# Cross attention's value projection in one sweep of 512 moving columns, and three side loads of the feed-forward stage queued behind weight loads

## The chip, the cores and the metric

The kernel runs on one core of a Trainium2 chip. The metric is the device time of one execution in microseconds (us); less is better. Every number of the trace comes from one profiled execution.

## What is computed

One inference step of a decoder trunk of one layer, for a prompt of 256 tokens and a batch of 8 single-token samples that share the parameters (264 token columns in all, D_MODEL 2048). Three sub-layers follow one another: attention beside a state-space scan, cross attention into 256 memory tokens, and a feed-forward block with a short convolution. The change lies in the second, with a small part in the third. The prompt's side of the second, cut to what matters (`rms_norm` scales a row by the inverse root of its mean square):

```
q = rms_norm(rms_norm(x, g) @ w_cq)      # 4 heads of 128
k = rms_norm(rms_norm(mem, g_mem) @ w_ck)
v = rms_norm(mem, g_mem) @ w_cv          # 256 memory tokens, 2048 -> 512
p = softmax(q @ k.T * scale)             # per head, 256 x 256
x = x + (p @ v) @ w_co                   # 512 -> 2048
```

The samples do the same with cached keys and values of their own.

## The kernel before, in words

TensorE works on float32 data as float32r. To keep the precision, every operand of a projection is split in two: `hi`, the value rounded to float32r, and `lo`, the rest. One logical product is then three matmul passes, hi by hi, hi by lo and lo by hi (`mm3`, L97 to L100). A weight streams in as parts of 128 x 1024 (512 KB). For each part `weights()` (L73 to L88) issues the load on SyncE's queue (L79), ScalarE casts it to `whi` (L85) and VectorE subtracts to get `wlo` (L86). The raw part, `whi` and `wlo` have four buffers each, so a load can start only when an old part has been split, and a split only when an old part's matmuls are done.

All engines run their own instructions in order. The order in which the Tile framework puts them there is decided by a scheduler at build time; work inside `tc.high_priority()` (the weight loads and splits, most evacuations) is put ahead of other work that is ready, and `tc.issue_after(i)` keeps an instruction behind another one of its own engine. PSUM, the accumulators of TensorE, is given out by tags: three banks for `mm`, two for `t`, and one each for `s`, `x` and `y`. A tile of a tag waits until an earlier tile's last reader has finished.

Cross attention on the prompt runs like this:

- `probs(h, f)` (L1050 to L1071) makes head h's softmax. Two matmuls put the logits in the only bank `s` (L1055); VectorE takes the row maximum (L1058) and scales it (L1059); ScalarE takes the exponential, one half at a time (L1063); VectorE takes the reciprocal of the sum (L1064) and multiplies (L1066); TensorE transposes the result in four pieces into a bank `t` (`tr`, whose matmul is L257); ScalarE copies it out to `pts` (L1071). In the rows of the order the copy's target is called `vp` or `pp`: names of buffers that it shares.
- `v_pair(i)` (L1074 to L1087) projects the memory tokens to the values of two heads: 2 weight units of 2 parts each, 8 slices of 128 rows a unit, 2 halves of the memory tokens, 3 passes of 256 moving columns. That is 96 passes a call. Here the memory tokens stand still as TensorE's stationary operand, and the weight moves. Two evacuations by ScalarE (L1087) of 128 x 256 each put the halves into `vx` (also called `vp`).
- `out_head(h)` (L1089 to L1095) multiplies values and probabilities: two matmuls (L1093) into bank `s` for odd heads and bank `y` for even ones, ScalarE's cast into `OH` (L1094) and VectorE's subtraction into `OL` (L1095). Both lie in one buffer named `ohl`.
- The calls: `probs` for heads 2 and 3, then `v_pair(0)`, `sample_out()` (the samples' outputs, which go through TensorE's banks `x` and `y` and end in the small splits at L93), `out_head` 0 and 1, `v_pair(1)`, `out_head` 2 and 3. Then `w_co` is applied: 8 parts, 264 moving columns a pass, into four banks `mm, mm, t, t` at first.

In the code's order the softmaxes stand ahead of all of the values. The scheduler puts passes of `v_pair` between a softmax's steps as they become ready, so in the built program the chains of heads 2 and 3 run while TensorE works through the values.

The feed-forward stage needs `fpast`, the samples' earlier rows (L1176), on GpSimd's `past()` (L1207 and the lines behind it). The stage also updates the samples' scan states in `new_state` (L1188 to L1200), a side job: each of 16 states is loaded as `hn` (L1194), every fourth one together with a broadcast row `bb` (L1192). These loads stand in the same SyncE queue as the weights.

Of the kernel before, what the change touches and what calls it, by code (L numbers as in the profile page):

```python
# [9 lines left out]
AF = mybir.ActivationFunctionType  # L10
# [5 lines left out]
KB = D // 128  # L16
# [31 lines left out]
def hybrid_decoder_step_kernel(ctx: ExitStack, tc: tile.TileContext, I, O):  # L48
    nc = tc.nc
# [16 lines left out]

    NPART, WBUFS = 1024, 4

    def raw_part(n=NPART):
        return wpool.tile([128, n], F32, tag="wraw", name="wraw", bufs=4)  # L70

    def weights(src, n=2048, into=None):

        out = []
        with tc.high_priority():
            for o in range(0, n, NPART):
                w = min(NPART, n - o)
                x = raw_part(w)
                nc.sync.dma_start(out=x, in_=src[:, o:o + w])  # L79
                if into:  # L80
                    hi, lo = into
                else:
                    hi = wpool.tile([128, w], F32R, tag="whi", name="whi", bufs=WBUFS)
                    lo = wpool.tile([128, w], F32R, tag="wlo", name="wlo", bufs=WBUFS)
                S.copy(out=hi, in_=x)  # L85
                V.tensor_tensor(out=lo, in0=x, in1=hi.bitcast(F32), op=ALU.subtract)  # L86
                out.append((hi, lo))
        return out  # L88
# [8 lines left out]
    def mm3(out, wh, wl, xh, xl, start, stop):  # L97
        PE.matmul(out, wh, xh, start=start, stop=False)  # L98
        PE.matmul(out, wh, xl, start=False, stop=False)  # L99
        PE.matmul(out, wl, xh, start=False, stop=stop)  # L100
# [298 lines left out]
    p = psum("y")  # L399
# [123 lines left out]
                              start=kb == 0, stop=kb == nb - 1)  # L523
            marks["attn"] = S.copy(out=attn[:, j, c * 128:c * 128 + 128], in_=o[:, 0:128])

    marks = {}
    pq = psum("s")
    for jj in range(4):
        in_pair(lambda m, pm: V.tensor_tensor(out=qT[:, 2 * jj + m, :], in0=pm, in1=r0, op=ALU.mult))
# [374 lines left out]
    def mem_hl(k):  # L904
        return mh[k // 8][:, k % 8, :TP], ml[k // 4][:, k % 4, :]
# [165 lines left out]
        S.copy(out=pts[h // 2][:, h % 2].rearrange("p a q -> p (a q)"), in_=p)  # L1071


    def v_pair(i):  # L1074
        pv = [psum("mm") for _ in range(2)]
        for u in range(2):
            parts = [w.rearrange("p (k c) -> p k c", c=256) for hl in weights(I["w_cv"][2 * i + u]) for w in hl]
            nk = parts[0].shape[1]
            for k in range(8):
                wh, wl = parts[2 * (k // nk)], parts[2 * (k // nk) + 1]  # L1080
                mhi, mlo = mem_hl(8 * u + k)
                for c in range(2):
                    cs = slice(c * 128, c * 128 + 128)
                    mm3(pv[c][:, 0:256], mhi[:, cs], mlo[:, cs], wh[:, k % nk, :], wl[:, k % nk, :],
                        u + k == 0, u == 1 and k == 7)
        for c in range(2):
            S.activation(out=vx[:, c, 256 * i:256 * i + 256], in_=pv[c][:, 0:256], func=AF.Copy, scale=rmc[:, 0, c:c + 1])  # L1087

    def out_head(h):  # L1089
        pt = pts[h // 2][:, h % 2]  # L1090
# [35 lines left out]
    nc.sync.dma_start(out=O["mem_k"], in_=kx)  # L1126
    for h in range(2, 4):
        probs(h, fq[1][:, :, h - 2])
    for i in range(2):
        v_pair(i)  # L1130
        if i == 0:
            sample_out()
        for m in range(2):
            out_head(2 * i + m)
    nc.sync.dma_start(out=O["mem_v"], in_=vx)

    X2 = [(T3(apool, 8, F32R, "B", f"x2h{h}", 4), T3(apool, 8, F32R, "B", f"x2l{h}", 4)) for h in range(2)]
# [35 lines left out]

    fp = ctx.enter_context(tc.tile_pool(name="fp", bufs=1))
    fpast = fp.tile([128, 2, 88, 8], F32, name="fpast")
    nc.sync.dma_start(out=fpast, in_=I["fpast"])  # L1176
    fnew = fp.tile([128, 88, 10], F32, name="fnew")

    fpc = fp.tile([128, 88, 8], F32, name="fpc")
# [32 lines left out]
    ffn = {}  # L1212
# [3 lines left out]
    def up(g):  # L1216
        H = (T3(apool, 8, F32R, "A", f"hh{g}", 4), T3(apool, 8, F32R, "A", f"hl{g}", 4))
        n = len(groups[g])
        for ii, i in enumerate(groups[g]):
            us = []  # L1220

            def ev(m, pm, i=i):
                bi = i + FB * m
                u = fp.tile([128, 2 + T], F32, tag="u", name="u", bufs=4)
                P.memset(u[:, 0:2], 0.0)
                ffn["ev"] = V.tensor_tensor(out=u[:, 2:], in0=pm, in1=r2, op=ALU.mult)
                us.append(u)

            proj([w_up[2 * i], w_up[2 * i + 1]], X2, ev, tag="t" if i % 2 else "mm")
            if i == 3:  # L1230
                past()
            cs = []
            for m in range(2):
                bi = i + FB * m
                u = us[m]
                P.tensor_copy(out=fnew[:, bi, :], in_=u[:, TP:])
                c = fp.tile([128, TP], F32, tag="c", name="c", bufs=4)
                w = [pc("fw", t * 88 + bi) for t in range(3)]
                ffn["c"] = S.activation(out=c, in_=u[:, 0:TP], func=AF.Identity, scale=w[0], bias=pc("fb", bi))
                for t in (1, 2):  # L1240
                    V.scalar_tensor_tensor(out=c, in0=u[:, t:t + TP], scalar=w[t], in1=c, op0=ALU.mult, op1=ALU.add)
                cs.append(c)
            if 4 <= i < 36:
                with tc.issue_after(ffn["ev"].ins), tc.issue_after(ffn["c"].ins):
                    new_state(i // 2 - 2, i % 2)
            S.activation(out=cs[0], in_=cs[0], func=AF.Silu)
            V.tensor_tensor(out=cs[1], in0=cs[0], in1=cs[1], op=ALU.mult)
            split(H[0][:, ii, :TP], H[1][:, ii, :TP], cs[1])
# [64 lines left out]
def _pack(np, x):  # L1313
# [30 lines left out]
    d["w_out"] = np.concatenate([units(wo[:1024][qperm], 8, 256), units(wo[1024:], 8, 256)])  # L1344
    d["w_cq"] = units(x["w_cq"][0], 8, 256)
    d["w_ck"] = units(x["w_ck"][0], 8, 256)
    d["w_cv"] = units(x["w_cv"][0], 8, 256)
    d["w_co"] = units(x["w_co"][0], 4, 512)
    wu = x["w_up"][0].reshape(D, 2, FB, 128).transpose(0, 2, 1, 3).reshape(D, 2 * DFF)
    d["w_up"] = units(wu, 8, 256)  # L1350
# [84 lines left out]
```

## Time and profile before

| what | value |
|---|---|
| timed, median of 3 runs | 1420.21 us (1420.08 to 1420.94) |
| the profiled execution, its whole time | 1417.36 us |
| its span (first to last instruction) | 1415.6 us, so 1.76 us lie around it |
| TensorE matmuls (PE) busy | 1404.7 us, 99% of the span |
| VectorE (DVE), ScalarE (ACT), GpSimd (POOL) busy | 1047.4, 767.4, 91.8 us |
| DMA, mean of all moved | 211 GB/s |
| share of the chain that ended last | PE 94%, DVE 3%, ACT 1%, DMA 1% |

PE is TensorE's matmuls, PEld its loads of the stationary operand, which run beside matmuls; SP is SyncE's queue. A matmul's duration in a row overlaps its neighbour's, since matmuls are pipelined: what a pass costs is the spacing of starts. Times from the span's start stand in the rows of the timeline and of the chain of waits, and the releaser of an idle time stands in square brackets behind the row that it delayed.

### The profile page before, as it was taken

What the parts mean: (1) busy time and instruction counts of PE and PEld (TensorE: products, weight loads), DVE (VectorE), ACT (ScalarE), POOL (GpSimd) and SP (SyncE); (2) the same over time, 40 slices, a digit from 0 to 9 for tenths busy, and PEclk for the clock granted to TensorE, in tenths of its full rate; (3) what the DMA queues carried; (4) which work ended last, traced back from release to release, by engine and by line L of the source; (5) the groups of instructions that cost most, each with busy time, mean ns of one, the idle gap of its engine ahead of it and who ended that gap; (6) DMA issues with size and microseconds to landing.
All of it is one profiled execution on the core that took longest, in us unless ns stands there. A gap on an engine that the chain in (4) does not pass through costs nothing.

```text
span 1415.6 us, 29115 instructions
## 1 busy us (share of the span) xinstructions
PE 1404.7 (99%) x11561; PEld 1375.8 (97%) x11561; DVE 1047.4 (74%) x1906; ACT 767.4 (54%) x1257; POOL 91.8 (6%) x277
## 2 busy tenths in 40 slices
PE   9999999999999999999999999999999999999999
PEld 9998899999999999899999999999999999999998
DVE  7859879999996875468677775777577757765664
ACT  6557765547645555557555553555355535543432
POOL 0000001211000000020010010001000100000000
PEclk9999999999999999999999999999999999999999
DMA  8863347777766557765566675666566655555554
GB/s 289 288 194 124 128 153 253 237 230 246 249 220 243 180 190 259 259 237 192 184 227 240 223 244 183 207 234 235 181 213 226 214 180 195 197 177 190 182 190 138
DMA packets 90487, 298.32 MB, mean 211 GB/s; under 512 B 12272, under 2 KB 17264, under 8 KB 89840
## 3 DMA queue, kind: packets, MB, share of 16 engines
q1 hardware_dynamic: 84560, 277.33, 57.5%
q0 software_dynamic: 5504, 18.88, 4.1%
q8 instruction: 90, 1.47, 0.4%
q14 instruction: 45, 0.37, 0.1%
q10 hardware_dynamic: 288, 0.27, 0.1%
HBM read 280.76 MB, written 16.23 MB: 210 GB/s over the span
## 4 chain that ended last, share of the span: by engine, by line
PE 94%; DVE 3%; ACT 1%; DMA 1%; issue 1%; ACTq 0%; DVEq 0%
PE mm L98 20%; PE mm L99 20%; PE mm L100 20%; PE t L98 9%; PE t L100 9%; PE t L99 9%; DVE wlo L86 1%; PE t L226 1%; PE s L493 1%; PE t L257 1%; ACT whi L85 1%; PE t L522 1%; PE y L713 0%; PE x L187 0%; DMA wraw<-in_w_in_dram 0%
## 5 line engine op out<-in xcount | busy, mean ns | idle before, releaser
L85 ACT CAST whi<-wraw 128x1024 fp32r<-128x1024 f32 x444 | 464.1, 1048 | 536.2 <-PE mm L99 289.6
L86 DVE TENSOR_TENSOR wlo<-wraw,whi 128x1024 fp32r<-128x1024 f32 x444 | 542.8, 1224 | 250.3 <-ACT whi L85 244.3
L98 PE MATMUL t<-x2h,whi 128*128 128x264 f32 x704 | 199.9, 284 | 0.0
L98 PE MATMUL mm<-x2h,whi 128*128 128x264 f32 x704 | 199.8, 284 | 0.0
L99 PE MATMUL t<-x2l,whi 128*128 128x264 f32 x704 | 199.8, 284 | 0.0
L99 PE MATMUL mm<-x2l,whi 128*128 128x264 f32 x704 | 199.6, 284 | 0.0
L100 PE MATMUL t<-x2h,wlo 128*128 128x264 f32 x704 | 199.5, 284 | 0.0
L100 PE MATMUL mm<-x2h,wlo 128*128 128x264 f32 x704 | 199.4, 283 | 0.0
L99 PE MATMUL mm<-hl,whi 128*128 128x264 f32 x704 | 198.7, 283 | 0.0
L100 PE MATMUL mm<-hh,wlo 128*128 128x264 f32 x704 | 198.2, 283 | 0.0
L98 PE MATMUL mm<-hh,whi 128*128 128x264 f32 x704 | 197.2, 284 | 0.0
L98 PE MATMUL mm<-xh,whi 128*128 128x264 f32 x608 | 175.5, 290 | 2.7 <-DVE t L328 1.8
L100 PE MATMUL mm<-xh,wlo 128*128 128x264 f32 x608 | 174.0, 290 | 0.4 <-DVE wlo L86 0.3
L99 PE MATMUL mm<-xl,whi 128*128 128x264 f32 x608 | 174.0, 287 | 0.0
L99 PEld LDWEIGHTS t<-x2l,whi 128*128 128x128 f32 x704 | 132.6, 188 | 0.0
L99 PEld LDWEIGHTS mm<-x2l,whi 128*128 128x128 f32 x704 | 132.5, 188 | 0.0
L99 PEld LDWEIGHTS mm<-hl,whi 128*128 128x128 f32 x704 | 132.5, 188 | 0.0
L98 PEld LDWEIGHTS mm<-x2h,whi 128*128 128x128 f32 x704 | 132.5, 188 | 0.0
L98 PEld LDWEIGHTS t<-x2h,whi 128*128 128x128 f32 x704 | 132.4, 188 | 0.0
L100 PEld LDWEIGHTS t<-x2h,wlo 128*128 128x128 f32 x704 | 132.2, 188 | 0.0
L100 PEld LDWEIGHTS mm<-x2h,wlo 128*128 128x128 f32 x704 | 132.1, 188 | 0.0
L100 PEld LDWEIGHTS mm<-hh,wlo 128*128 128x128 f32 x704 | 131.9, 188 | 0.0
(460 smaller groups left out, 2936.1 us busy)
## 6 DMA issues: line engine op xcount, KB each, us to landing
wraw<-in_w_up_dram SPq DMA_DIRECT2D x176, 512.0 KB, 3.9
wraw<-in_w_in_dram SPq DMA_DIRECT2D x102, 512.0 KB, 4.4
wraw<-in_w_dn_dram SPq DMA_DIRECT2D x88, 512.0 KB, 3.9
wraw<-in_w_out_dram SPq DMA_DIRECT2D x48, 512.0 KB, 4.3
h<-in_h_dram POOLq DMA_DIRECT2D x32, 256.0 KB, 4.5
hn<-in_h_dram SPq DMA_DIRECT2D x16, 512.0 KB, 5.0
out_state_s_dram<-hn POOLq DMA_DIRECT2D x16, 512.0 KB, 3.3
e<-dram_la SPq DMA_DIRECT2D x16, 256.0 KB, 5.1
```

What stands on the lines that cost most here:

```text
L85: S.copy(out=hi, in_=x)
L86: V.tensor_tensor(out=lo, in0=x, in1=hi.bitcast(F32), op=ALU.subtract)
L98: PE.matmul(out, wh, xh, start=start, stop=False)
L99: PE.matmul(out, wh, xl, start=False, stop=False)
L100: PE.matmul(out, wl, xh, start=False, stop=stop)
L226: PE.matmul(first[m][:, :T], w[:, m * 128:(m + 1) * 128], x, start=k + i == 0, stop=k == KB - 1 and i == 2)
L257: PE.transpose(out, in_, cst[0:k, C_ID:C_ID + k])
L493: PE.matmul(s3, qT[:, j, c * 128:c * 128 + 128], kbd[:, pp, :, 0:nk], start=True, stop=True)
L522: PE.matmul(o[64 * h:64 * h + 64, 0:128], vn[:, kb, pp, 64 * h:64 * h + 64], pt[:, h * nb + kb, :], start=kb == 0, stop=kb == nb - 1)
```

## The change

It has two parts.

The first makes one function, `values()`, of the two calls of `v_pair`. The host packs `w_cv` into 4 units with 512 columns in place of 8 with 256 (the bytes and the number of parts stay the same: 8 parts of 512 KB). A pass moves 512 columns, all four heads, and there are 4 units x 2 parts x 2 slices x 2 halves x 3 = 96 passes in place of 192. The sums fill two whole banks `mm`, and two evacuations of 128 x 512, now of high priority, replace four of 128 x 256. `sample_out()` is issued in the middle of `values()`, and all four `out_head` calls stand behind it.

The second notes the last weight load (`marks["load"]`) and keeps `fpast`'s load behind the last weight load issued so far, and each `new_state`'s `hn` and `bb` loads behind the last load of the `w_up` pair of their step.

```diff
-                nc.sync.dma_start(out=x, in_=src[:, o:o + w])
+                marks["load"] = nc.sync.dma_start(out=x, in_=src[:, o:o + w])
...
-    def v_pair(i):
+    def values():
         pv = [psum("mm") for _ in range(2)]
-        for u in range(2):
-            parts = [w.rearrange("p (k c) -> p k c", c=256) for hl in weights(I["w_cv"][2 * i + u]) for w in hl]
-            nk = parts[0].shape[1]
-            for k in range(8):
-                wh, wl = parts[2 * (k // nk)], parts[2 * (k // nk) + 1]
-                mhi, mlo = mem_hl(8 * u + k)
-                for c in range(2):
-                    cs = slice(c * 128, c * 128 + 128)
-                    mm3(pv[c][:, 0:256], mhi[:, cs], mlo[:, cs], wh[:, k % nk, :], wl[:, k % nk, :],
-                        u + k == 0, u == 1 and k == 7)
+        for u in range(4):
+            if u == 2:
+                sample_out()
+            for pi, hl in enumerate(weights(I["w_cv"][u])):
+                wh, wl = (w.rearrange("p (k c) -> p k c", c=512) for w in hl)
+                for k in range(2):
+                    kk = 4 * u + 2 * pi + k
+                    mhi, mlo = mem_hl(kk)
+                    for c in range(2):
+                        cs = slice(c * 128, c * 128 + 128)
+                        mm3(pv[c], mhi[:, cs], mlo[:, cs], wh[:, k, :], wl[:, k, :], kk == 0, kk == KB - 1)
         for c in range(2):
-            S.activation(out=vx[:, c, 256 * i:256 * i + 256], in_=pv[c][:, 0:256], func=AF.Copy, scale=rmc[:, 0, c:c + 1])
+            with tc.high_priority():
+                S.activation(out=vx[:, c, :], in_=pv[c], func=AF.Copy, scale=rmc[:, 0, c:c + 1])
...
-    for i in range(2):
-        v_pair(i)
-        if i == 0:
-            sample_out()
-        for m in range(2):
-            out_head(2 * i + m)
+    values()
+    for h in range(4):
+        out_head(h)
...
-    nc.sync.dma_start(out=fpast, in_=I["fpast"])
+
+    with tc.issue_after(marks["load"].ins):
+        nc.sync.dma_start(out=fpast, in_=I["fpast"])
...
             proj([w_up[2 * i], w_up[2 * i + 1]], X2, ev, tag="t" if i % 2 else "mm")
+            ffn["load"] = marks["load"]
...
-                with tc.issue_after(ffn["ev"].ins), tc.issue_after(ffn["c"].ins):
+                with tc.issue_after(ffn["ev"].ins), tc.issue_after(ffn["c"].ins), tc.issue_after(ffn["load"].ins):
                     new_state(i // 2 - 2, i % 2)
```

In the changed kernel the lines have moved: those of `weights`, `mm3`, `tr` and `split` by 2 (a high part's cast is L87, its low part L88, `mm3` L100 to L102, a transpose L259, the samples' small splits L95), `probs` by 1 (logits L1056, maximum L1059, its scaling L1060, exponential L1064, reciprocal L1065, multiplication L1067, copy L1072), the evacuation of the values is L1090 and `out_head`'s lines are L1096 to L1098.

The order of the built program moves at three places. The first is the softmax of the last head, head 3. On PE before, its logits (L1055) and head 2's transposes (`t<-cst,e`) stand among the passes of the second `v_pair`:

```order
L98 MATMUL mm<-whi,mh_5635 128x256
L99 MATMUL mm<-wlo,mh_5635 128x256
L1055 MATMUL s<-qk 128x256 x2
L100 MATMUL mm<-whi,ml 128x256
L98 MATMUL mm<-whi,mh_5635 128x256
L257 MATMUL t<-cst,e 128x128
L99 MATMUL mm<-wlo,mh_5635 128x256
L100 MATMUL mm<-whi,ml 128x256
L257 MATMUL t<-cst,e 128x128 x3
L98 MATMUL mm<-whi,mh_5635 128x256
L99 MATMUL mm<-wlo,mh_5635 128x256
```

On PE in the changed kernel, from the last two of the 96 passes to the first pass of `w_co` (`mm<-ohl,whi`); `s<-vp` and `y<-vp` are `out_head`s of heads 1 and 0, and the second set of `t<-cst,e` are head 3's transposes:

```order
L101 MATMUL mm<-wlo,mh_5635 128x512
L102 MATMUL mm<-whi,ml 128x512
L259 MATMUL y<-cst,rs 128x128
L1056 MATMUL s<-qk 128x256 x2
L259 MATMUL t<-cst,e 128x128 x4
L1096 MATMUL s<-vp 128x256 x2
L1096 MATMUL y<-vp 128x256 x2
L259 MATMUL t<-cst,e 128x128 x4
L100 MATMUL mm<-ohl,whi 128x264 x2
```

The logits of head 3 have moved behind the last pass of the values, and with them all that follows from them; no pass of a projection stands between them and the last transposes.

The second place is the same stretch on ACT and DVE of the changed kernel. On ACT, from the exponential of head 2 to the cast of head 0's output; L1090 are the evacuations of the values, L87 is the cast of a `w_co` part:

```order
L1064 ACTIVATE e,st<-s,st,hr 128x256 x2
L1090 ACTIVATE vp<-mm,rmc 128x512 x2
L87 CAST whi<-wraw 128x1024
L95 CAST ohl<-y 128x4x4
L1072 COPY pp_6768<-t 128x512
L1064 ACTIVATE e,st<-s,st,hr 128x256 x2
L95 CAST ohl<-y 128x4x4
L1097 CAST ohl<-s 128x256
L1097 CAST ohl<-y 128x256
```

On DVE of the changed kernel, from head 2's reciprocal to head 3's multiplication:

```order
L1065 RECIPROCAL st<-st 128x2
L1067 TENSOR_SCALAR e<-e,st 128x256 x2
L1059 TENSOR_REDUCE st<-s 128x2
L88 TENSOR_TENSOR wlo<-wraw,whi 128x1024
L1060 SCALAR_TENSOR_TENSOR st<-st,hr 128x2
L95 TENSOR_TENSOR ohl<-y,ohl 128x4x4
L1065 RECIPROCAL st<-st 128x2
L95 TENSOR_TENSOR ohl<-y,ohl 128x4x4
L1067 TENSOR_SCALAR e<-e,st 128x256 x2
```

Between head 3's maximum (L1059) and its scaling (L1060) stands the low part of a `w_co` part (L88), whose cast (L87) stands on ACT behind the evacuations of the values. The exponential of head 3 stands behind all of these. Before, DVE also had such a low part between the two, but the cast that it needs stood ahead of everything else there.

The third place is SyncE's queue, from the `w_co` loads to the first `w_up` loads. Before:

```order
L79 DMA wraw<-in_w_co_dram 128x1024 x3
L1176 DMA fpast<-in_fpast_dram 128x1408
L1192 DMA bb<-dram_bc 128x1024
L1194 DMA hn<-in_h_dram 128x1024 x2
L1135 DMA out_mem_v_dram<-vp 128x1024
L1194 DMA hn<-in_h_dram 128x1024
L79 DMA wraw<-in_w_co_dram 128x1024
L1192 DMA bb<-dram_bc 128x1024
L79 DMA wraw<-in_w_up_dram 128x1024 x32
```

And in the changed kernel:

```order
L81 DMA wraw<-in_w_co_dram 128x1024
L1135 DMA out_mem_v_dram<-vp 128x1024
L81 DMA wraw<-in_w_co_dram 128x1024
L1178 DMA fpast<-in_fpast_dram 128x1408
L81 DMA wraw<-in_w_up_dram 128x1024 x20
L1194 DMA bb<-dram_bc 128x1024
L1196 DMA hn<-in_h_dram 128x1024
L81 DMA wraw<-in_w_up_dram 128x1024 x8
L1196 DMA hn<-in_h_dram 128x1024
```

`fpast`, three states and two broadcast rows no longer stand ahead of the last `w_co` load; `fpast` comes right behind it, the first state 20 `w_up` loads later. On PE, ACT, DVE and POOL the feed-forward stage's own order is the same in both kernels.

More of the change, by code (lines that the diff above doesn't have):

```diff
@@ L67, in hybrid_decoder_step_kernel @@
     NPART, WBUFS = 1024, 4
+    marks = {}
     def raw_part(n=NPART):
@@ L524, in attn_prompt @@
             marks["attn"] = S.copy(out=attn[:, j, c * 128:c * 128 + 128], in_=o[:, 0:128])
-    marks = {}
     pq = psum("s")
@@ L1346, in _pack @@
     d["w_ck"] = units(x["w_ck"][0], 8, 256)
-    d["w_cv"] = units(x["w_cv"][0], 8, 256)
+    d["w_cv"] = units(x["w_cv"][0], 4, 512)
     d["w_co"] = units(x["w_co"][0], 4, 512)
```

## The prediction

> **What bounds the kernel now.** I read the head of the profile's page first: how busy each engine is.
>
> ```profile
> span 1415.6 us, 29115 instructions
> ...
> PE 1404.7 (99%) x11561; PEld 1375.8 (97%) x11561; DVE 1047.4 (74%) x1906; ACT 767.4 (54%) x1257; POOL 91.8 (6%) x277
> ```
>
> TensorE is the bound. An edit gains only what it takes from PE's passes or from the 11 us in which PE stands still, and loses what it adds to either. So next comes the table of windows, for PE alone: the values with what runs between them (582 to 618), the seam into `w_co` (618 to 627), the rest of `w_co` (to 660), the feed-forward stage.
>
> ```profile
> core 0: us, PE busy (x), PEclk, DMA share, GB/s
> 582.40:601.70 19.30, 19.30 (x165) 1.00 0.47 161
> 601.70:618.00 16.30, 16.30 (x130) 1.00 0.44 148
> 618.00:627.00 9.00, 8.13 (x61) 1.00 0.88 310
> 627.00:660.00 33.00, 33.00 (x273) 1.00 0.65 236
> 660.00:1413.00 753.00, 752.13 (x6210) 1.00 0.60 203
> ```
>
> PE has no gap in the value stage. It loses 9.00 - 8.13 = 0.87 us at the seam, and 753.00 - 752.13 = 0.87 us in the whole feed-forward stage. The list of what PE waited for names the longest stop of the program and the one at the seam.
>
> ```profile
> PE t L98 <- DVE u L778: 2.0, 1, 2.0
> ...
> PE mm L99 <- DVE ohl L1095: 0.9, 1, 0.9
> ```
>
> Only the second lies where the change does. The chain of waits shows how it comes about, and also what the steps of a head take on PE (logits 0.86 us, three transposes 0.33).
>
> ```profile
> 609.28 0.86 PE s L1055 x4
> ...
> 617.58 0.33 PE t L257 x3
> ...
> 619.86 2.04 issue
> 621.90 1.06 ACT whi L85
> 622.98 1.65 DVE wlo L86
> 624.63 0.34 DVE ohl L1095
> 625.02 0.39 PE mm L99
> ```
>
> A `w_co` part is cast late (621.90), its low part (622.98) stands on DVE ahead of the low part of a head's output (624.63), and PE's pass on that output (625.02) waits. For the 2.04 us ahead of the cast the profile names no releaser; they fall in the stretch with the DMA share of 0.88. In the changed order `fpast` and the states' loads are gone from ahead of the last `w_co` load, and the cast stands elsewhere, so I count the 0.87 us as removed; if the stop stays, the sum is 0.87 higher.
>
> **The passes.** 192 passes of 256 columns become 96 of 512. What a pass costs is the spacing of starts. Here are the first and the last of 22 passes without a gap, and, from the chain of waits, two fp32 records of 512 columns in an earlier stage (the four in the row at 609.28 have 256).
>
> ```profile
> 604.29 0.28 PE L99 MATMUL mm<-wlo,mh 128*128 128x256 f32 x1
> ...
> 606.77 0.30 PE L99 MATMUL mm<-wlo,mh 128*128 128x256 f32 x1
> ```
>
> ```profile
> 103.17 0.86 PE s L493 x2
> ```
>
> (606.77 - 604.29) / 21 = 0.118 us; I round it down to 0.117, so the 192 take 22.5 us. No float32r pass of 512 columns is in the trace. One end: it costs two of the old ones, 0.234, and nothing is gained. The other end comes from fp32. There a record of 256 columns takes 0.86 / 4 = 0.215 and one of 512 takes 0.43, just double. The float32r pass of 256 takes a little over half of its fp32 record, so half of 0.43, 0.215, is the least I can argue for 512: 96 x 0.215 = 20.6, a gain of 1.8. I take the middle, 0.224, since the 0.0095 us by which 0.117 exceeds half of 0.215 looks like a cost of the pass, not of the column: 96 x 0.224 = 21.5, **a gain of 1.0**.
>
> The Trainium skill's page "TensorE: Matmul & The Clock Gate" (Part 1, "Wait — 56ns, not 53.3ns?") puts a warm pass at N / 2.4 GHz plus 2.5 ns, 215.7 ns for 512 columns; by that alone the gain would be 1.8 and the sum 0.8 lower. For 256 columns the same rule gives 109 ns where the row has 118, so the rule is under the measurement here, and the measurement decides.
>
> **The tail of the values.** This is the largest term. The order shows head 3's logits, before, among the passes of the second projection; now they come behind the last pass, and no projection is left to cover the softmax. Let time 0 be the end of the last pass on PE. PE then has the samples' transpose (0.11), head 3's logits (0.86) and head 2's four transposes (0.44), and is through at 1.41. Next stands head 1's output, which goes into bank `s`. There is one such bank, and head 3's logits lie in it until ACT has taken their exponential. What ACT and DVE have to do first is in these rows, from the timelines of ACT and of DVE.
>
> ```profile
> 612.20 0.56 ACT L1063 ACTIVATE e<-s,st,hr 128x256 f32<-128x256 f32 x1 [0.51 <-DVE st L1059]
> ...
> 613.20 0.20 ACT L1063 ACTIVATION_READ_ACCUMULATOR e<-s,st,hr 128x1 f32 x1
> ...
> 617.42 0.48 ACT L1087 ACTIVATE vp<-mm,rmc 128x256 f32<-128x256 f32 x1
> 617.94 0.59 ACT L1071 COPY pp<-t 128x512 f32<-128x512 f32 x1
> ```
>
> ```profile
> 612.01 0.15 DVE L1059 SCALAR_TENSOR_TENSOR st<-st,hr 128x2 f32<-128x2 f32 x1
> ...
> 614.37 1.23 DVE L86 TENSOR_TENSOR wlo<-wraw,whi 128x1024 fp32r<-128x1024 f32 x1
> ```
>
> ACT begins its evacuations 0.2 after time 0: a pass lasts 0.16 beyond the start of the next (0.28 less 0.118), and a handoff from engine to engine takes 0.04 (DVE's scaling ends at 612.16, ACT starts at 612.20). An evacuation of 128 x 512 is not in the trace. ACT's copy of that size took 0.59, two evacuations of half the size would be 2 x 0.48 = 0.96; I take 0.70, nearer to the copy, which has the same shape. Two end at 1.6. ACT's cast of the `w_co` part (1.06 in the chain's row) ends at 2.66, DVE's low part (0.04 and 1.23) at 3.93, head 3's scaling (0.15), which stands behind it on DVE, at 4.1. The exponential's two halves take 613.40 - 612.20 = 1.2 and end at 5.3. PE starts head 1's output at 5.35: it has **stood still for 5.35 - 1.41 = 3.9 us**.
>
> Behind that PE has the outputs of heads 1 and 0 (0.86 each, to 7.07) and head 3's transposes (to 7.51, their inputs done on DVE meanwhile). The first pass of `w_co` needs ACT's cast of head 0, from 7.1 on; it has the size of the 0.48 us evacuation, so PE perhaps waits 0.1 or 0.2 more. So the tail has 4.1 us of standing still. With evacuations of 0.59 and no wait at `w_co` it is 3.7; with 0.96, and a low part as slow as that at 622.98 (1.65 for 1.23, in the stretch in which side loads land), it is 4.1 + 0.5 + 0.4 = 5.0. Evacuations of high priority don't shorten it: they open this chain already.
>
> **The side loads.** In the changed order `fpast` goes right behind the last `w_co` load, the first state behind 20 `w_up` loads. These rows are from the DMA issues, SP's timeline and the matmuls of the feed-forward stage's first operand.
>
> ```profile
> hn<-in_h_dram SPq DMA_DIRECT2D x16, 512.0 KB, 5.0
> ```
>
> ```profile
> 624.66 92.55 SPq L79 DMA_DIRECT2D wraw<-in_w_up_dram  x32
> ```
>
> ```profile
> L98 PE MATMUL mm<-x2h,whi x704: 280/284/291, 644.2 to 1330.2; 128*128 128x264 f32 x176
> ```
>
> A state lands in 5.0 us. A weight load runs about 644.2 - 624.66 = 19.5 us ahead of its matmuls, and a state's load now goes out with the loads of its own step, so it lands some 14 us before that step's matmuls begin. The updates on ACT and DVE come behind these. PE's waits in 753 us are 0.87 us together, so the feed-forward part can gain no more than that, and I cost it at 0. Without that cover ACT would stand still for up to 5.0 us per state with the weight casts behind it. `out_mem_v`, now ahead of the last `w_co` load, waits for the evacuations until 1.6; that load needs a raw part which the low part above releases at 3.93 only, so the wait costs nothing.
>
> **The sum.** 4.1 (new tail) - 0.9 (stop at the seam) - 1.0 (passes) = **+2.2 us**. The profiled execution took 1417.36, so it would take 1419.6. The timed runs' median, 1420.21, lies 2.85 above it; with the same distance I forecast **1422.4**. What can be told from no change is 0.2%, 2.8 us, so 1417.4 to 1423.0 is the same. The bounds: 3.7 - 0.9 - 1.8 = +1.0, and 5.0 - 0.9 - 0 = +4.1, which is 1421.2 to 1424.3.
>
> **The rivals.**
>
> *The clock falls (slower, 0.10).* If PE stands still for 4 us, the chip may lower the granted clock, and PE starts again slowly. Two rows of the chain of waits give the price: PE's first 16 records of the program, and two warm ones of the same 264 columns.
>
> ```profile
> 1.20 6.42 PE x L187 x16
> ...
> 659.74 0.45 PE y L274 x2
> ```
>
> 16 x 0.225 = 3.6 would be the warm time, so 2.8 us are lost: +5.0, **1425.2**. Against it: the longest stop in the program, 2.0 us, is shorter, and no trace here shows where the clock falls. It decides if the window over the tail shows a clock under 1.00. The Trainium skill (the same page, Part 1) has the clock halved after an idle window of 3.4 us that runs free of the program. By that rule a stop of 3.9 us would seldom hold a whole window; no trace here shows it.
>
> *Wide passes cost two narrow ones (slower, 0.15).* The gain of 1.0 is gone: +3.2, **1423.4**. For it: the 0.0095 us may belong to the columns. Against it: fp32 passes show no cost per pass at all.
>
> *The tail is mostly covered (same, 0.15).* If DVE gets to head 3's scaling before the low part, or a cast waits less than I have it, the exponential starts behind the cast, at 2.7 in place of 4.1, and the stop falls by 1.4: +0.8, **1421.0**; with passes of 0.215 as well, 0.0, 1420.2. Against it: each engine takes its instructions in the order that is written, and the low part stands ahead.
>
> *Much cheaper passes (faster, 0.03).* The Trainium skill's page also states about 131 ns for sustained passes of 512 columns ("Back-to-back issue gap"). As a mechanism here: if a pass's cost were mostly a fixed one, 512 columns would cost little more than 256. At 0.13 the 96 passes take 12.5, a gain of 10.0: -6.8, **1413.4**. Against it: the fp32 rows double from 256 to 512 columns, 0.215 to 0.43.
>
> *The side loads bite or pay (0.05).* A stop per state, as above, for a few of the 16 states: +1 to +5, or the 0.87 us of the feed-forward stage gained.
>
> My forecast has the rest, 0.52. Faster is 0.04: the cheap passes and a little of the covered tail. Slower is the clock 0.10, the wide passes 0.15, half of the side loads and a seventh of my own case, where its terms near the upper ends: 0.35. The same is left with 0.61. The range runs from 1419.8, a covered tail with cheap passes less half of the 0.9 between the timed runs, to 1425.0, just under the clock's case; that leaves out the clock, the cheap passes and some of the side loads.
>
> **What would show it.** In the changed profile: starts of 512-column passes 0.224 apart, and 96 of them in about 21.5 us; one stop of about 3.9 us on PE ahead of head 1's output, released by ACT's exponential, with the evacuations, the cast, the low part and the scaling in that order ahead of it; the stop at the first passes of `w_co` under 0.3; a granted clock of 1.00 in that window; waits in the feed-forward stage still under 1 us. A stop under 2 us there, spacing under 0.2 or over 0.24, or new waits behind 660 us would prove me wrong.

## The result and the profile after

The changed kernel takes 1422.16 us (median of 20 runs, 1420.14 to 1425.04), the kernel before, run beside it, 1419.41 (20 runs, 1416.91 to 1421.18). The ratio is 1.0022, 95% interval 1.0016 to 1.0028: 2.75 us slower. The forecast was 1422.4 and +2.2. The time fits more closely than the step: the base that I added the step to, 1420.21, was 0.8 above the median of 20 runs.

The head of the page after, beside which the page before stands in the prediction:

```profile
span 1420.5 us, 28939 instructions
...
PE 1408.1 (99%) x11465; PEld 1373.5 (97%) x11465; DVE 1049.0 (74%) x1906; ACT 767.6 (54%) x1255; POOL 92.4 (7%) x277
```

PE has 96 passes fewer and yet is busy for 3.4 us more. The windows of PE, over the same stretches as before:

```profile
core 0: us, PE busy (x), PEclk, DMA share, GB/s
582.40:601.70 19.30, 19.30 (x116) 1.00 0.49 170
601.70:618.00 16.30, 15.43 (x77) 1.00 0.50 150
618.00:627.00 9.00, 7.01 (x34) 0.81 0.59 210
627.00:660.00 33.00, 33.00 (x271) 1.00 0.44 142
660.00:1413.00 753.00, 753.00 (x6219) 1.00 0.63 208
```

Two things are new: 2.86 us of standing still across 618, and a granted clock of 0.81 behind it. The feed-forward stage has no stop at all. The timeline of PE, from the last ten of the wide passes to head 0's output and on to the first pass of `w_co`, shows both:

```profile
613.22 0.40 PE L102 MATMUL mm<-whi,ml 128*128 128x512 f32 x1
...
615.32 0.40 PE L102 MATMUL mm<-whi,ml 128*128 128x512 f32 x1
615.55 0.27 PE L259 MATMUL y<-cst,rs 128*128 128x128 f32 x1
...
619.99 1.77 PE L1096 MATMUL s<-vp 128*128 128x256 f32 x4 [2.86 <-ACT ohl L95]
621.55 1.91 PE L1096 MATMUL y<-vp 128*128 128x256 f32 x4
...
623.93 0.51 PE L100 MATMUL mm<-ohl,whi 128*128 128x264 f32 x2
```

Head 1's output stands where the prediction has the stop. Its releaser is named as ACT's small cast at L95, which stands right behind the exponential on ACT. The chain of waits has the steps ahead of it:

```profile
613.00 1.05 ACT whi L87
614.04 1.10 ACT e L1064 x4
615.15 0.59 ACT vp L1090
615.78 0.56 issue
616.34 1.04 ACT whi L87
617.41 1.23 DVE wlo L88
618.74 1.20 ACT e L1064 x4
620.01 1.75 PE s L1096 x4
621.76 1.71 PE y L1096 x4
623.47 0.64 PE t L259 x4
```

Evacuations, cast, low part and exponential come in the forecast order; the scaling (L1060) lies in the gap ahead of 618.74. Heads 1 and 0 take 1.75 and 1.71 us, where a head's output took 0.86 before. The windows of one us each say why:

```profile
core 0: us, PE busy (x), PEclk, DMA share, GB/s
...
619.00:620.00 1.00, 0.01 (x1) 1.00 0.91 332
620.00:621.00 1.00, 1.00 (x3) 0.67 0.77 270
621.00:622.00 1.00, 1.00 (x4) 0.50 0.60 221
622.00:623.00 1.00, 1.00 (x4) 0.50 0.24 90
623.00:624.00 1.00, 1.00 (x7) 0.62 0.00 0
624.00:625.00 1.00, 1.00 (x8) 1.00 0.00 0
```

PE runs at half clock for some 3 us. What that costs is best seen beside the experiment `a_only` (below), which has a stop of the same length at the same place and a clock of 1.00 behind it:

```profile
620.72 1.13 PE L1096 MATMUL s<-vp 128*128 128x256 f32 x4 [2.87 <-ACT ohl L95]
...
623.17 0.50 PE L100 MATMUL mm<-ohl,whi 128*128 128x264 f32 x2
```

From head 1's output to the first pass of `w_co` it takes 623.17 - 620.72 = 2.45 us there and 623.93 - 619.99 = 3.94 us here, so this fall costs 1.5 us.

A third new thing is smaller. The samples' outputs (L1037 before, L1038 now) are the same 32 records in both kernels. The windows with these instructions alone, before and after:

```profile
590.00:612.00 22.00, 3.85 (x32) 1.00 0.42 144
```

```profile
590.00:612.00 22.00, 4.68 (x32) 1.00 0.35 116
```

That is 0.83 us more, and PE's timeline shows why. The stationary operand of each of these records has 32 columns (`128*32`) where a full one has 128, and mostly four of them run side by side, a step every 0.43 us. In both kernels head 1's transposes split the block: before, behind 8 records, two full steps; now behind 26, so that two records are left to run one behind the other alone:

```profile
601.85 1.02 PE L1038 MATMUL x<-va,pz 128*32 128x512 f32 x2
```

The last six then run three at a time. That makes ten steps in place of eight, and two steps of 0.43 are the 0.83.

From the first pass of the values (582.4 before, 583.0 after) to the first pass of the feed-forward stage (644.2, 649.1) it is 4.3 us longer in these two traces: 2.86 - 0.87 = 2.0 of standing still, 1.5 of clock, 0.8 of the samples' outputs, and nothing left over. In `a_only`, whose clock doesn't fall in this stretch, it is 2.9 longer (583.7 to 648.4): the same without the clock. Neither is the difference of the medians, because the clock doesn't fall at the same places in every execution. Each execution's mean clock is on record to three decimals (not for the 20 runs of before beside the changed kernel), so the executions with 1.000 can be set side by side:

| kernel | median us | ratio, 95% interval | executions at clock 1.000 | their mean us |
|---|---|---|---|---|
| before, beside the first four experiments | 1419.36 | | 7 of 33 | 1418.25 |
| before, beside the next four | 1419.14 | | 9 of 33 | 1418.30 |
| before, beside the last three | 1419.29 | | 4 of 20 | 1417.88 |
| changed | 1422.16 | 1.0022, 1.0016 to 1.0028 | 5 of 20 | 1420.55 |
| `a_only` | 1422.29 | 1.0020, 1.0011 to 1.0029 | 2 of 11 | 1420.64 |
| `b_only` | 1421.95 | 1.0017, 1.0008 to 1.0026 | 0 of 11 | |
| `filler` | 1422.00 | 1.0019, 1.0010 to 1.0028 | 3 of 11 | 1421.10 |
| `narrow_late` | 1419.12 | 0.9995, 0.9987 to 1.0004 | 3 of 11 | 1417.77 |
| `b_states` | 1419.66 | 1.0002, 0.9993 to 1.0011 | 5 of 11 | 1418.31 |
| `b_fpast_late` | 1418.77 | 0.9998, 0.9989 to 1.0007 | 4 of 11 | 1417.85 |
| `sout_last` | 1420.60 | 1.0009, 1.0000 to 1.0017 | 3 of 11 | 1418.66 |
| `narrow_fpast` | 1418.18 | 0.9995, 0.9986 to 1.0004 | 4 of 11 | 1417.52 |
| `xbank` | 1422.49 | 1.0026, 1.0017 to 1.0036 | 1 of 10 | 1420.42 |
| `stop_long3` | 1424.73 | 1.0042, 1.0030 to 1.0055 | 0 of 5 | |
| `narrow_all` | 1417.85 | 0.9992, 0.9984 to 1.0001 | 5 of 11 | 1417.06 |

One of the 11 executions of `narrow_fpast` took 1954.39 us at a mean clock of 0.654; its ratio leaves that one out.

At full clock the change costs 1420.55 - 1418.25 = 2.3 us by these means, of 5 and 7 executions, and 2.9 by the trace of `a_only`. So most of the 2.75 is standing still and the samples' outputs. The mean clock over the changed kernel's executions is 0.99840, that of before 0.99891 in the 33 beside the first experiments; the clock's share in the medians is thus some tenths of a us, and these runs don't settle it more closely.

### The profile page after: what moved, and what is told of

It is laid out like the page before. It is cut to its first block, busy times and chain, and to the rows that moved or that the text cites. A ratio compares the mean times of both kernels' runs of the same rounds, so it can differ in the third digit from the quotient of the medians.

```text
span 1420.5 us, 28939 instructions
## 1 busy us (share of the span) xinstructions
PE 1408.1 (99%) x11465; PEld 1373.5 (97%) x11465; DVE 1049.0 (74%) x1906; ACT 767.6 (54%) x1255; POOL 92.4 (7%) x277
## 4 chain that ended last, share of the span: by engine, by line
PE 96%; DVE 1%; ACT 1%; DMA 1%; issue 0%; ACTq 0%; DVEq 0%
PE mm L100 21%; PE mm L101 21%; PE mm L102 21%; PE t L100 9%; PE t L102 9%; PE t L101 9%; DMA e<-dram_la 1%; PE t L228 1%; PE s L495 1%; PE t L259 1%; PE t L524 1%; PE y L714 1%; PE x L189 0%; ACT whi L87 0%; PE y L730 0%
## 5 line engine op out<-in xcount | busy, mean ns | idle before, releaser
L87 ACT CAST whi<-wraw 128x1024 fp32r<-128x1024 f32 x444 | 464.3, 1048 | 542.3 <-PE mm L101 292.7
L88 DVE TENSOR_TENSOR wlo<-wraw,whi 128x1024 fp32r<-128x1024 f32 x444 | 544.6, 1228 | 249.7 <-ACT whi L87 242.0
L100 PE MATMUL t<-x2h,whi 128*128 128x264 f32 x704 | 199.8, 284 | 0.0
L100 PE MATMUL mm<-x2h,whi 128*128 128x264 f32 x704 | 199.8, 284 | 0.0
L102 PE MATMUL t<-x2h,wlo 128*128 128x264 f32 x704 | 199.6, 284 | 0.0
L102 PE MATMUL mm<-x2h,wlo 128*128 128x264 f32 x704 | 199.3, 283 | 0.0
L102 PE MATMUL mm<-hh,wlo 128*128 128x264 f32 x704 | 198.2, 283 | 0.0
L100 PE MATMUL mm<-hh,whi 128*128 128x264 f32 x704 | 197.2, 284 | 0.0
L100 PE MATMUL mm<-xh,whi 128*128 128x264 f32 x608 | 176.0, 291 | 3.2 <-DVE t L330 1.9
L102 PE MATMUL mm<-xh,wlo 128*128 128x264 f32 x608 | 174.6, 291 | 0.4 <-DVE wlo L88 0.3
L100 PEld LDWEIGHTS mm<-x2h,whi 128*128 128x128 f32 x704 | 132.5, 188 | 0.0
L100 PEld LDWEIGHTS t<-x2h,whi 128*128 128x128 f32 x704 | 132.4, 188 | 0.0
L102 PEld LDWEIGHTS t<-x2h,wlo 128*128 128x128 f32 x704 | 132.2, 188 | 0.0
L102 PEld LDWEIGHTS mm<-x2h,wlo 128*128 128x128 f32 x704 | 132.1, 188 | 0.0
L102 PEld LDWEIGHTS mm<-hh,wlo 128*128 128x128 f32 x704 | 132.0, 188 | 0.0
```

## The experiments

**The two parts apart: `a_only` and `b_only`.** The first is the changed kernel with the side loads where they were, the second the kernel before with the side loads moved.

```diff
-    with tc.issue_after(marks["load"].ins):
-        nc.sync.dma_start(out=fpast, in_=I["fpast"])
+    nc.sync.dma_start(out=fpast, in_=I["fpast"])
...
-                with tc.issue_after(ffn["ev"].ins), tc.issue_after(ffn["c"].ins), tc.issue_after(ffn["load"].ins):
+                with tc.issue_after(ffn["ev"].ins), tc.issue_after(ffn["c"].ins):
```

> The wide value projection alone; fpast, the states and the broadcast rows are loaded where they were before. Theory 1 (a stop of 2.9 us at the softmax of head 3, and a lower clock for some 3.4 us behind it, are the loss): slower than before by about what the whole change costs, 2.5 to 3.5 us, with one PE stop of 2.5 to 3.5 us ahead of head 1's output. Rival (the moved side loads cost something): within 1 us of before. If the side loads ahead of the last w_co load still delay it, a second stop of up to 1 us stands in the w_co stage, and the kernel is up to 1 us slower than the whole change.

> The queue order of the side loads alone, with the values in two narrow projections as before. PE, ACT, DVE and POOL have the instructions of before in the order of before. Theory 1: between 0 and 0.9 us faster than before, since at most the stop of 0.87 us at the first w_co passes goes; no new stop in the feed-forward stage. Rival (the moved side loads are the loss): slower than before by 2 us or more.

`a_only` takes what the whole change takes, with a stop of 2.9 us at the same place. The list of what its PE waited for:

```profile
PE s L1096 <- ACT ohl L95: 2.9, 1, 2.9
```

So the projection accounts for the loss. But `b_only` is slower too, by about 2.6 us: my theory of the side loads falls, and they are neither free nor a gain. The two losses don't add up: together they cost what either costs alone. PE's timeline in `b_only` has a stop in the middle of `w_co` that neither kernel has, and the timelines of POOL and DVE show what goes on then:

```profile
638.17 0.39 PE L100 MATMUL t<-ohl,whi 128*128 128x264 f32 x1 [1.34 <-DVE res L1143]
```

```profile
629.46 1.42 POOL L1209 TENSOR_TENSOR fpc<-fpast,par 128x704 f32<-128x704 f32 x1 [9.76 <-DMA fpast<-in_fpast_dram]
...
635.17 1.50 POOL L1212 TENSOR_TENSOR fpc<-fpc,par 128x704 f32<-128x704 f32 x1
```

```profile
629.93 1.24 DVE L97 SCALAR_TENSOR_TENSOR x2l<-res,par,x2h 128x264 fp32r<-128x264 f32 x1
631.09 2.44 DVE L88 TENSOR_TENSOR wlo<-wraw,whi 128x1024 fp32r<-128x1024 f32 x1
633.46 0.42 DVE L1143 TENSOR_TENSOR res<-mm,res 128x264 f32<-128x264 f32 x1
633.80 3.97 DVE L97 SCALAR_TENSOR_TENSOR x2l<-res,par,x2h 128x264 fp32r<-128x264 f32 x4
...
638.37 0.48 DVE L97 SCALAR_TENSOR_TENSOR x2l<-res,par,x2h 128x264 fp32r<-128x264 f32 x1
```

GpSimd works on `fpast` from 629.5 to 636.7, and DVE's instructions stretch to double and more: `x2l` 1.24 and about 1.0 each for 0.48, a low part 2.44 for 1.23. Adding `res` out of PSUM stays at 0.42. Then PE waits for DVE. The Trainium skill's page "SBUF — State Buffer" ("SBUF: two separate sides") says that DVE and GpSimd share a pair of ports under an exclusive lock, and that a DVE instruction with two inputs in SBUF is among those that block, against a GpSimd instruction that reads SBUF. The rows agree: `x2l` and `wlo` have two such inputs, `res` one.

The stop accounts for a part of the loss. From the first pass of the values to the first of the feed-forward stage `b_only` takes 2.1 us more than before, 1.5 of it standing still: this stop, another of 0.6 at the feed-forward stage's first pass, less 0.4 at the seam. Of the 11 executions none has the clock at 1.000, and their mean is 0.99782; what lowers it isn't shown, as this profile has no fall behind the stop.

Before, GpSimd's work on `fpast` ran from 622.1 to 629.2 and was all but over when the first `x2l` came, at 629.1. This made a second theory: what costs in the side loads is the moment at which `fpast` lands, not the states.

**`fpast` or the states: `b_states` and `b_fpast_late`.** The first is `b_only` with `fpast`'s load as before; the second loads it behind the third `w_up` pair (the edit below, against `b_only`).

```diff
-    with tc.issue_after(marks["load"].ins):
-        nc.sync.dma_start(out=fpast, in_=I["fpast"])
...
+            if i == 2:
+                with tc.issue_after(marks["load"].ins):
+                    nc.sync.dma_start(out=fpast, in_=I["fpast"])
             if i == 3:
                 past()
```

> The queue order of the states and broadcast rows alone; fpast is loaded ahead of the last w_co load as before, the values are narrow as before. Theory 2 (what costs in the side loads alone is fpast: GpSimd's work on it, some 7 us, then falls on DVE's evacuations of w_co and stretches them): within 0.8 us of before, w_co's evacuations (x2l on DVE) near 0.48 us each, no PE stop over 0.9 us in the w_co stage. Rival (the states' later loads are what costs): slower than before by 1.8 us or more, as with both.

> The side loads moved as in the change, but fpast goes still later, behind the third w_up pair, so that GpSimd works on it in the feed-forward stage; the values are narrow as before. Theory 2: the loss of 2.6 us goes; between 1 us faster than before and 0.5 us slower, no PE stop over 0.6 us in the w_co stage and none of more than 0.5 us where GpSimd now works. Rival (the loss moves along with GpSimd's work): a PE stop of 1 to 2 us in the feed-forward stage and 1.8 us or more slower than before.

Both come out as theory 2 has it: 1.0002 and 0.9998, where `b_only` has 1.0017. In `b_fpast_late` GpSimd starts at 668.2, beside the feed-forward stage, and PE has no stop from there on; the longest stop of the `w_co` stage is 0.5. In `b_states` the stop of 0.9 us at the seam is still there, in the list of waits:

```profile
PE mm L101 <- DVE ohl L1096: 0.9, 1, 0.9
```

So that stop isn't due to the states' and broadcast rows' loads being where they were. It is 0.5 in `b_only` and `b_fpast_late`, where `fpast`'s load too went behind the last `w_co` load.

In the changed kernel GpSimd's work (from 628.2) falls earlier within `w_co`, whose first pass is late by the stop: two low parts stretch (2.05 and 2.10 us), but the evacuations come mostly behind it and no PE stop follows. In `a_only` too `fpast`'s load goes out behind the last `w_co` load, and by SP's list of waits it waits for head 3's transposes (L259) in both kernels, 3.5 us in `a_only` and 5.1 in the changed one; GpSimd starts at 627.4, 0.8 before the changed kernel's. So with the wide projection the second part hardly moves `fpast`, and it costs nothing on top of the first.

**Late outputs without wide passes: `narrow_late`.**

```diff
         v_pair(i)
         if i == 0:
             sample_out()
-        for m in range(2):
-            out_head(2 * i + m)
+    for h in range(4):
+        out_head(h)
```

> The kernel before with one edit: all four outputs of the heads stand behind the second narrow projection, as in the change; passes of 256 columns stay. Head 3's logits stay among the passes in the order. Theory 1 (the loss is that head 3's softmax lost its cover): within 1 us of before, with no PE stop over 1.2 us at this place and a clock of 1.00 there. Rival (that the outputs stand behind the values is itself the loss): slower than before by 2 us or more.

0.9995: no loss, and no stop ahead of the outputs. That the outputs stand behind the values costs nothing; head 3's softmax behind the last pass does. The stop of 0.87 us at the seam is gone here as well, though the side loads are where they were; one of 0.5 stands at the feed-forward stage's first pass.

**Filling the stop: `filler`.**

```diff
+    d = psum("x")
+    with tc.issue_after(marks["lg"].ins):
+        for j in range(6):
+            PE.matmul(d[:, 0:256], qx[:, 0, 0:128], kx[:, 0, :], start=True, stop=True)
     for h in range(4):
         out_head(h)
```

> The changed kernel with six more fp32 matmuls of 256 columns (0.43 us each, 2.6 us in all) into the free bank x, behind head 3's logits; nobody reads their result. They fill the stop with work that is thrown away and shorten nothing that ACT and DVE do. Theory 1 with the clock: PE has no stop over 0.5 us there, the clock stays at 1.00, heads 1 and 0 take 0.86 us each, and the kernel is 1 to 2 us faster than the changed one, so 1 to 2.2 us slower than before. Rival (only the stop counts, the clock doesn't matter): the same time as the changed kernel, within 0.4 us. Rival 2 (the exponential is delayed by something that the matmuls share): slower than the changed kernel by up to 2.6 us.

PE's longest stop there is 0.3 us and the clock is 1.00 at this place, but the gain of 1 to 2 us isn't there: the median is 0.2 under the changed kernel's, within the noise, as the rival in the expectation has it. The trace says why so little was to be gained. From the first pass of the values to the first of the feed-forward stage `filler` takes 64.8 us, `a_only` with its stop 64.7: the discarded matmuls take as long as the stop did, and only a fall of the clock, 1.5 us where it comes (66.1 in the changed kernel), can be saved. The executions' mean clock is 0.99900 in place of 0.99840, which is 0.8 us of PE's 1405 us of busy time. But the executions at full clock are 0.55 us slower (1421.10 to 1420.55, three against five, and one of the three is at 1422.10), and differences this small aren't clear of the noise. What the clock behind this stop costs on average stays open; it is less than 1.5 us, since `a_only` shows that the fall doesn't always come.

**A longer stop: `stop_long3`.** Each evacuation of the values is done three times over.

```diff
             with tc.high_priority():
-                S.activation(out=vx[:, c, :], in_=pv[c], func=AF.Copy, scale=rmc[:, 0, c:c + 1])
+                for _ in range(3):
+                    S.activation(out=vx[:, c, :], in_=pv[c], func=AF.Copy, scale=rmc[:, 0, c:c + 1])
```

> The changed kernel with each evacuation of the values done three times, four times 0.7 us more on ScalarE; PE has the same instructions in the same order, and its stop ahead of head 1's output grows by about 2 us, from 2.9 to 4.5 to 5.2. Theory of the clock (the longer PE stands still, the more often the clock falls behind it): heads 1 and 0 take 1.7 us each in the profile in place of 0.86, few or none of the executions show a mean clock of 1.000, and the kernel is 2.4 to 3.8 us slower than the changed one. Rival (the falls of the clock have nothing to do with this stop): slower than the changed kernel by the 2 us alone, with as many executions at 1.000 as it had, 5 in 20.

The median is 2.6 us over the changed kernel's, none of 5 executions shows 1.000, and the profile has the half clock behind the stop:

```profile
622.38 2.07 PE L1097 MATMUL s<-vp 128*128 128x256 f32 x4 [4.27 <-ACT ohl L95]
624.25 1.58 PE L1097 MATMUL y<-vp 128*128 128x256 f32 x4
```

The stop is 1.4 us longer, less than the 2 I expected, so 1.2 us are left, which the clock could explain. With 5 executions against 20 this points to the theory without settling how often the clock falls.

**Another bank: `xbank`.**

```diff
-        o = psum("s" if h % 2 else "y")
+        o = psum("x" if h % 2 else "y")
```

> The changed kernel with the outputs of heads 1 and 3 in bank x in place of bank s, so that head 1's output no longer waits for the exponential of head 3. Theory 1: the softmax still has no cover, so the stop moves on and shrinks: no stop ahead of head 1's output, one of 1.5 to 2.3 us ahead of head 3's transposes, released by DVE's multiplication; 0.4 to 1.5 us faster than the changed kernel, 1.2 to 2.4 us slower than before. Rival (the single bank s is the whole cause): no stop over 0.5 us, within 0.7 us of before.

Both expectations missed: no gain, 1.0026. The stop moved, but to head 0's output, which waits for bank `y`:

```profile
620.08 1.18 PE L1096 MATMUL y<-vp 128*128 128x256 f32 x4 [2.36 <-DVE ohl L95]
```

Bank `y` holds the samples' transposed outputs until DVE's small splits (L95) have read them, and these stand on DVE behind head 3's scaling. So the single bank `s` isn't the whole cause; what is uncovered is the row of ACT's and DVE's steps, and with either bank the release lies near its end. Free banks for both heads weren't tried. An estimate from this trace: DVE's multiplication for head 3 ends at 620.5 and PE would be through with both heads' outputs at about 618.4, so head 3's transposes would still wait some 2 us.

**Real work in the stop: `sout_last`.**

```diff
-            if u == 2:
-                sample_out()
...
     values()
+    sample_out()
     for h in range(4):
         out_head(h)
```

> The changed kernel with the samples' outputs issued behind the wide projection in place of in its middle, so that their matmuls, some 3.5 us, stand between the last pass and head 3's logits and cover a part of the softmax. Theory 1: the stops between the last pass and w_co fall to 1.2 to 2.2 us in all, and the kernel is 0.5 to 2 us faster than the changed one, so 0.8 to 2.5 us slower than before. Rival (the chain moves with the logits): the stop stays at 2.9 us and the time is that of the changed kernel within 0.4 us.

The samples' matmuls cover part of the chain. The stops ahead of `w_co` are 1.0 + 0.6 us in the list of waits:

```profile
PE s L1094 <- ACT ohl L95: 1.0, 1, 1.0
PE y L259 <- DVE rs L1043: 0.6, 1, 0.6
```

The samples' outputs, no longer split, are also faster than in either kernel, by the same window as above:

```profile
590.00:622.00 32.00, 3.64 (x32) 1.00 0.54 178
```

1.0009 in place of 1.0022, and 1.9 us less at full clock. By the traces 2.86 - 1.6 = 1.3 of standing still and 4.68 - 3.64 = 1.0 of the samples' outputs make 2.3. With the same 96 wide passes about half of the loss is gone.

**What is left to gain: `narrow_fpast` and `narrow_all`.** Both are `narrow_late` with `fpast` behind the third `w_up` pair; the second also has the states' loads moved.

> No wide projection and no moved states: the kernel before with the heads' outputs behind both narrow projections and fpast's load behind the third w_up pair. Theories 1 and 2 together: faster than before by 0.5 to 1.5 us, with stops between 600 and 660 us of 0.7 us in all or less. Rival (the remaining stops have other causes): within 0.5 us of before, with 0.8 us or more of stops left there.

> The kernel with narrow projections, the heads' outputs behind both of them, the states' loads moved as in the change, and fpast's load behind the third w_up pair: what the other runs point to. Theories 1 and 2: faster than before by 0.5 to 1.4 us, with stops of 0.5 us or less in all between 600 and 660 us. Rival (nothing is left to gain there): within 0.4 us of before.

Their medians lie 1.0 and 1.4 us under those of before, the means at full clock 0.8 each, but both intervals reach 1. PE's windows in `narrow_all`, the seam and the rest of `w_co`:

```profile
618.00:627.00 9.00, 8.87 (x61) 1.00 0.55 177
627.00:660.00 33.00, 33.00 (x274) 1.00 0.52 169
```

0.13 us of standing still is left here, 0.74 less than before and near the 0.8 at full clock. Against the changed kernel `narrow_all` is 4 us faster; against before a gain under 0.2% is likely and not proved.

## Why the prediction was right, and where its terms were off

**The bound.** Right: what counted was PE's passes and stops, and the order on ACT, DVE and POOL only where PE waited for it.

**The passes.** The step that took the middle, 0.224, failed. Ten wide passes start from 613.22 to 615.32, (615.32 - 613.22) / 9 = 0.233 apart, which is all but the upper end, 0.234. A pass of 512 columns costs two of 256. The gain is 192 x 0.117 - 96 x 0.233 = 0.1 us, not 1.0; the rival "wide passes cost two narrow ones" was right on this term. The two figures for 512 columns that the prediction cites from the Trainium skill's page "TensorE: Matmul & The Clock Gate", 215.7 ns (Part 1, "Wait — 56ns, not 53.3ns?") and 131 ns ("Back-to-back issue gap"), don't hold for these float32r passes: 233 ns were measured.

**The tail.** The mechanism was right: softmax without cover, the wait for bank `s`, and evacuations, cast, low part, scaling and exponential in the forecast order. Only the size was off: 4.1 us forecast, 2.86 measured. The step that failed is "ACT begins its evacuations 0.2 after time 0". Time 0 is 615.55 here. The evacuations begin at 615.05, 0.5 ahead of it: the first of them needs only one half of the memory tokens, whose last pass stands three passes, 0.7 us, before the end. This is 0.7 of the 1.2; 0.2 was the wait at `w_co`, and some 0.2 is counting, since the profile's 2.86 runs from the modelled end of the last transpose (617.13) and mine from where the next pass could start. The evacuations take 0.70 each, as I had it (1.39 for two in ACT's timeline, the row below). Behind them each step took about what the rows of before gave. The 0.1 or 0.2 of waiting at `w_co` can't be read here, where PE ran at half clock up to that point.

```profile
615.05 1.39 ACT L1090 ACTIVATE vp<-mm,rmc 128x512 f32<-128x512 f32 x2
```

**The seam.** Right in the changed kernel: the 0.87 us are gone. Of the two reasons given, the order is the one that counts: `narrow_late` loses the stop with the side loads where they were, and `b_only` keeps 0.5 of it with the side loads moved.

**The side loads.** Costed at 0, and on top of the projection they do cost 0 (`a_only`). But the working was wrong. It looked at the states' loads and at SP's queue and left out who works on `fpast` when it lands: alone the part costs a ratio of 1.0017, through the moment at which GpSimd works on `fpast`, beside DVE's evacuations. I put the 1.65 us low part (622.98) down to side loads landing; by the rows of `b_only` it is GpSimd's work on `fpast`, which began at 622.1.

**The samples' outputs** took 0.8 us more, two steps of 0.43. The prediction put them at nothing, though `sample_out()` moves.

**The clock.** The prediction counted on 1.00 in that window, and the changed kernel's profile has 0.81 there: this sign failed. The rival's price of 2.8 was too high, since the fall costs 1.5, and not in every execution. It was read from the program's first records, over which the profile shows a clock of 1.00, so it wasn't shown to be a price of the clock. My argument against the rival was that the longest stop, 2.0 us, was shorter; but the clock falls behind stops of that length too (below), which the rule that the prediction cites from the Trainium skill's page (Part 1), an idle window of 3.4 us, doesn't cover.

**The sum.** At full clock the traces give 2.0 (stop) + 0.8 (samples' outputs) - 0.1 (passes) = 2.7 (2.9 by the whole stretch in `a_only`) and the medians 2.75, beside my 4.1 - 0.9 - 1.0 = 2.2. That the two are so near is in part luck: a tail that I had 1.2 too long stood against passes that gained 0.9 too much and a term of 0.8 that I had missed. The change lies at the 0.2% that I took as the limit of "the same".

## What to carry to other kernels

When two projections become one, ask what stood between them: the scheduler had used the passes as cover for the softmax of the last heads, and the cheapest check was to follow the last head's chain through the order. A load that is queued later also moves the engine that works on it, and where that engine and the one that PE waits for slow each other, as GpSimd and DVE did here, this can cost more than the load. A stop of TensorE of about 2 us can cost more than its length, since the clock is sometimes halved for some 3 us behind it. Work that has to be done anyhow, put into the stop, shortens it (`sout_last`); work that is thrown away doesn't (`filler`).

## What the runs showed of the hardware

I had not expected that the clock falls behind stops this short. A stop near 38 us is in every kernel here, 1.8 us long in nearly all. 7 of the 13 profiles have a fall behind it, with 0.57 to 0.73 in the window from 40 to 44. The changed kernel's:

```profile
40.00:44.00 4.00, 4.00 (x21) 0.57 0.97 372
```

Before is among the 6 without one, and its profiled execution, 1417.36, lies near the fast end of its runs. A stop near 402 us is 2.0 us long in 10 profiles, and behind it the clock fell in 3 of them, for example in `narrow_late`:

```profile
404.00:408.00 4.00, 3.70 (x17) 0.57 0.72 201
```

Behind the stop at the values' end it fell in the changed kernel (2.86 us), `xbank` (2.36) and `stop_long3` (4.27), and didn't in `a_only` (2.9). So the length alone doesn't decide, and what does isn't shown. In windows of 4 us over the whole of each profile the clock is below 1.00 at these three places only, and no stop under 1.8 us was followed by a fall. An execution with a mean clock 0.001 lower takes about 1 us longer: 1.0 by a line through the 33 executions of before beside the first experiments, 0.9 through the 20 of the changed kernel. These lines account for half and two thirds of the variance between runs of one kernel.
